# Attention pipeline of a two-layer decoder trunk: weight units parted one per quarter, two query copies for three, the heads' normalisation shared by ScalarE and GpSimd

## The chip, the cores and the metric

The kernel runs on one core of a Trainium2 chip. The metric is the time of one execution on the device, in microseconds (us): the median of the runs. A core has engines that work side by side, each through its own instructions in order, and wait for each other by semaphores: TensorE (PE in the profile, its weight loads PEld), VectorE (DVE), ScalarE (ACT), GpSimd (POOL), and SyncE (SP), which issues the DMAs here. TensorE writes its results to PSUM, from where VectorE and ScalarE fetch them.

## The reference

A trunk of two layers over 256 positions of width 1024, in float32, batch 1. Each layer is half a SwiGLU, a mixer, half a SwiGLU, each between RMS norms. The first layer's mixer is a causal pooling, the second's an attention whose keys and values come from the residual stream after the first layer. What the change touches is this mixer:

```python
def dilated_mixer(h, cos, sin, w_q, k_sh, v_sh, w_o):
    q = (h @ w_q).reshape(B, S, N_ATTN_GROUPS, HEADS_PER_GROUP, HEAD_DIM)   # 3 groups, 8 heads, 64
    q = apply_rope(q, cos, sin)
    for g, (window, dilation) in enumerate(ATTN_GROUPS):
        o, l = dilated_window_attention(q[:, :, g], k_sh[:, :, g], v_sh[:, :, g], window, dilation)
    ...
    wts = jax.nn.softmax(jnp.stack(lses, axis=0), axis=0)
    o = jnp.sum(wts[..., None] * jnp.stack(outs, axis=0).astype(jnp.float32), axis=0)
    return o.reshape(B, S, O_WIDTH) @ w_o
```

Each group has its own mask (which keys a query sees). Weighting the three outputs by the softmax of their log denominators is the same as one softmax over the keys of all three groups together, and the kernel computes that.

## The kernel before, in words

Float32 products are made from two rounded halves: every weight and every activation is split into a high part and a residual, and three matmuls (high by high, high by residual, residual by high) make one product. So every piece of weight that is loaded passes through ScalarE, which casts the high part (L99), and VectorE, which subtracts it to get the residual (L100). `parts(raw, k)` does this for one unit: half of a loaded buffer of two units. A unit of the query weights is 768 columns wide, a unit of all other weights 1024. Loaded buffers (`raw`) come in three, formed units (`hl`) in six, with two more in a pool `xy`.

The attention stage comes after the keys and values are projected. The positions lie in two tiles of 128 rows (`i` = 0, 1), the eight heads in four pairs (`pr` = 0 to 3), and a pair has an even head (`e` = 0) and an odd one (`e` = 1). For each `pr` and `i` there are these steps:

- `q_proj(pr, i, half)`: projects the queries of a pair for all three groups (384 columns) in two halves of two units each; after the second half, `rope` on VectorE (L658 to L662: product, two half products, sum).
- `q_turn(pr, i)`: three transposes on TensorE (`qtp`), copied by ScalarE to the transposed queries `qT` (L772).
- `scores(pr, i)`: the scores of both heads on TensorE (`sc`), on VectorE the mask and the row maximum (L710), on ScalarE the exponential with the row sum `den` (L714; the profile shows the reading of the sum as an instruction of its own, ACTIVATION_READ_ACCUMULATOR).
- `over_sums(pr, i)`: for each head the reciprocal of the sum on VectorE (L720), and the probabilities `p` scaled by it in place on GpSimd (L721).
- `p_turn(pr, i)`: four transposes for each head on TensorE (`ptp`), each head's copied by ScalarE (L737).
- `values(pr, i)`: sixteen matmuls with the values (`ob`), whose result goes to `oT`, high part by ScalarE (L748), residual by VectorE (L749).
- `next_q(pr, k)`, called once in each quarter k of a `pr`: loads the weights of the next pair (the output weights in the last `pr`) and forms their units.

The loop over `pr` mixes the steps of neighbouring pairs, written out by hand. A `pr` issues in this order: `q_proj(pr,0,0)`, `over_sums(pr-1,0)`, `q_turn(pr-1,1)`, `p_turn(pr-2,1)`, `next_q(pr,0)`, `q_proj(pr,0,1)`, `scores(pr-1,1)`, `values(pr-2,1)`, `p_turn(pr-1,0)`, `next_q(pr,1)`, `q_proj(pr,1,0)`, `over_sums(pr-1,1)`, `q_turn(pr,0)`, `values(pr-1,0)`, `next_q(pr,2)`, `q_proj(pr,1,1)`, `scores(pr,0)`, `next_q(pr,3)`. After the loop come the output projection `o_proj` and the last steps of the last pairs. The loop lies in a region (`manual_schedule`) in which TensorE, VectorE and ScalarE issue the region's instructions in the order in which the code emits them; GpSimd and the DMA queue are ordered by the compiler's scheduler, which also decides where instructions from outside the region (the first weight units of the next SwiGLU, for one) fall between them.

Of the kernel before, what the change touches and what calls it, by code (L numbers as in the profile page):

```python
# [19 lines left out]
P = 128  # L20
# [27 lines left out]
def trunk_kernel(ctx: ExitStack, tc: tile.TileContext, x, pos, gains, pscale, ws, wq, invf, amask, pmat, icnt, out):  # L48
    nc = tc.nc
# [36 lines left out]
    def load_raw(pool=rawp, tag="raw", raw=None, at=None):  # L86

        b = block_no[0]
        raw = pool.tile([P, 2, 1024], F32, tag=tag, name=f"{tag}{b}") if raw is None else raw
        for k in range(2) if at is None else (at,):  # L90
            last["dma"] = nc.sync.dma_start(raw[:, k], ws[b, :, k * 1024 : (k + 1) * 1024])
        block_no[0] += at != 0
        return raw

    def parts(raw, k, n=1024, xy=False):

        pool, tag = (xyp, "xy") if xy else (hlp, "hl")
        hl = pool.tile([P, 2, 1024], F32R, tag=tag, name="hl")
        nc.scalar.copy(hl[:, 0, :n], raw[:, k, :n])  # L99
        last["dve"] = nc.vector.tensor_sub(hl[:, 1, :n], raw[:, k, :n], hl[:, 0, :n])  # L100
        return hl[:, 0], hl[:, 1]
# [8 lines left out]
    def load_units(n, xy=False):  # L110

        units = []
        for b in range(n // 2):
            raw = load_raw()
            units += [parts(raw, k, xy=xy and b == 0) for k in range(2)]
        return units
# [1 line left out]
    def load_form():  # L118
        return form(load_raw())

    def load_q_units(pr, b):
        raw = rawp.tile([P, 2, 1024], F32, tag="raw", name=f"rawq{pr}{b}")
        nc.sync.dma_start(raw[:, :, :768], wq[pr * 2 + b])
        return [parts(raw, k, 768, pr % 2 == 0 and b == 0) for k in range(2)]

    def mm(o, l, r, start, stop):
        nc.tensor.matmul(o, l, r, start=start, stop=stop)  # L127
# [357 lines left out]
    with tc.manual_schedule(engines={mybir.EngineType.DVE, mybir.EngineType.Activation}):  # L485
        y = norm(0, gpre, "x")
        raws = [load_raw(at=0)]
# [59 lines left out]
    raw = rawp.tile([P, 2, 1024], F32, tag="raw", name="rawpm")  # L547
# [4 lines left out]
    units = load_units(8, True)  # L552
# [58 lines left out]
    units = load_units(8, True)  # L611
# [41 lines left out]
    def rope(src, i, nh, name):  # L653
        r = sc2.tile([P, nh, 2, 32], F32, tag="w2", name=f"ra_{name}")
        b = sc2.tile([P, nh, 2, 32], F32, tag="w2", name=f"rb_{name}")
        s4 = src.rearrange("p (h two d) -> p h two d", two=2, d=32)
        c4 = ctab[:, i : i + 1].to_broadcast([P, nh, 2, 32])
        nc.vector.tensor_mul(r, s4, c4)  # L658
        for z in range(2):
            sz = stab[:, i, z : z + 1].to_broadcast([P, nh, 32])  # L660
            nc.vector.tensor_mul(b[:, :, z], s4[:, :, 1 - z], sz)
        nc.vector.tensor_add(r, r, b)  # L662
        return r.rearrange("p h two d -> p (h two d)")
# [6 lines left out]
    for g in range(3):  # L670
        units = load_units(4, g % 2 == 0)
        for i in range(2):
            ps = gup.tile([P, 512], F32, tag="gu", name=f"kp{g}{i}")
            proj_mm(ps, hkT, i, units, 512)
            r = rope(ps, i, 8, f"k{g}{i}")
            tp = tpp.tile([P, 4, P], F32, tag="tp", name=f"ktp{g}{i}")
# [3 lines left out]
    for g in range(3):  # L680
        units = load_units(4, g % 2 == 1)
# [5 lines left out]
    qx = [s8p.tile([P, 2, 1024], F32, tag="s8", name=f"qT{k}") for k in range(2)]  # L687
    qx.append(s4p.tile([P, 2, 512], F32, tag="s4", name="qT2"))
    qT = [qx[g // 2][:, g % 2].rearrange("p (r s) -> p r s", r=4) for g in range(3)]
    am = qx[2][:, 0].bitcast(BF16).rearrange("p (i k) -> p i k", i=2)  # L690
    pTt = [t.rearrange("p (c t) -> p c t", c=4) for t in (qx[1][:, 1, 0:512], qx[1][:, 1, 512:1024], qx[2][:, 1])]
    nc.gpsimd.dma_start(am, amask.rearrange("i p k -> p i k"))
# [3 lines left out]
    def scores(pr, i, pool=accp, tag="acc"):  # L696

        q = [t[:, pr] for t in qT]
        t = slice(i * P, (i + 1) * P)
        sc = [pool.tile([P, 512], F32, tag=tag, name=f"sc{i}_{pr}{e}") for e in range(2)]  # L700
        for o, g, keys in ((0, 0, slice(0, S)), (256, 1, t), (384, 2, t)):
            for e in range(2):
                a = slice(e * 64, e * 64 + 64)
                n = keys.stop - keys.start
                mm(sc[e][:, o : o + n], q[g][a, t], kT[g][a, pr, keys], True, True)
        probs[i, pr] = []
        for e in range(2):
            p = sc2.tile([P, 512], F32, tag="w2", name=f"p{i}_{pr}{e}")
            mx = st.tile([P, 1], F32, tag="mx", name=f"mx{i}_{pr}{e}")
            nc.vector.tensor_tensor_reduce(p, sc[e], am[:, i], 1.0, -3.0e38, op0=ALU.add, op1=ALU.max, accum_out=mx)  # L710
            nm = st.tile([P, 1], F32, tag="nm", name=f"nm{i}_{pr}{e}")
            nc.vector.tensor_scalar_mul(nm, mx, -0.125)
            den = st.tile([P, 1], F32, tag="den", name=f"den{i}_{pr}{e}")
            nc.scalar.activation(p, p, AF.Exp, bias=nm, scale=0.125, accum_out=den)  # L714
            probs[i, pr].append((p, den))

    def over_sums(pr, i):
        for e, (p, den) in enumerate(probs[i, pr]):
            rd = st.tile([P, 1], F32, tag="rd", name=f"rd{i}_{pr}{e}")
            nc.vector.reciprocal(rd, den)  # L720
            nc.gpsimd.tensor_scalar_mul(p, p, rd)  # L721
            probs[i, pr][e] = p

    oT = [None, None]
# [3 lines left out]
    def p_turn(pr, i):  # L728

        pT[i, pr] = []  # L730
        for e in range(2):
            tp = tpp.tile([P, 4, P], F32, tag="tp", name=f"ptp{i}_{pr}{e}")
            for c in range(4):
                nc.tensor.transpose(tp[:, c], probs[i, pr][e][:, c * P : (c + 1) * P], ident)
            pT[i, pr].append(pTt[npt[0] % len(pTt)])
            npt[0] += 1
            nc.scalar.copy(pT[i, pr][e], tp)  # L737
# [15 lines left out]
    def o_proj(i, chunks):  # L753
        if chunks[0] == 0:
            acc_f[i] = acc_pair(f"o{i}")
        for k in chunks:
            row_mm(acc_f[i], oT[i][:, 0, k], oT[i][:, 1, k], units[k], k == 0, k == 3)

    def q_proj(pr, i, half, units):
        if half == 0:  # L760
            qp[i] = accp.tile([P, 512], F32, tag="acc", name=f"qp{pr}{i}")
        for q in (2 * half, 2 * half + 1):
            proj_mm(qp[i][:, :384], aT, i, units, 384, only=q)
        if half == 1:
            qr[pr, i] = rope(qp[i][:, :384], i, 6, f"q{pr}{i}")

    def q_turn(pr, i):
        tp = gup.tile([P, 4, P], F32, tag="gu", name=f"qtp{pr}{i}")
        for c in range(3):
            nc.tensor.transpose(tp[:, c], qr[pr, i][:, c * P : (c + 1) * P], ident)  # L770
        for g in range(3):
            nc.scalar.copy(qT[g][:, pr, i * P : (i + 1) * P], tp[:, g])  # L772

    qp, qr = {}, {}
    units = []

    def next_q(pr, k):

        if k % 2 == 0:
            units.extend(load_q_units(pr + 1, k // 2) if pr < 3 else load_units(2))  # L780

    with tc.manual_schedule(engines={mybir.EngineType.PE}):
        with tc.manual_schedule(engines={mybir.EngineType.DVE, mybir.EngineType.Activation}):
            units += load_q_units(0, 0) + load_q_units(0, 1)
            for pr in range(4):
                cur, units = units, []
                q_proj(pr, 0, 0, cur)
                if pr > 0:
                    over_sums(pr - 1, 0)
                    q_turn(pr - 1, 1)  # L790
                if pr > 1:
                    p_turn(pr - 2, 1)
                next_q(pr, 0)
                q_proj(pr, 0, 1, cur)
                if pr > 0:
                    scores(pr - 1, 1)
                if pr > 1:
                    values(pr - 2, 1)
                if pr > 0:
                    p_turn(pr - 1, 0)  # L800
                next_q(pr, 1)
                q_proj(pr, 1, 0, cur)
                if pr > 0:
                    over_sums(pr - 1, 1)
                q_turn(pr, 0)
                if pr > 0:
                    values(pr - 1, 0)
                next_q(pr, 2)
                q_proj(pr, 1, 1, cur)
                scores(pr, 0)  # L810
                next_q(pr, 3)
        o_proj(0, (0,))
        over_sums(3, 0)
        q_turn(3, 1)
        o_proj(0, (1, 2))
        p_turn(3, 0)
        scores(3, 1, gup, "gu")
        values(3, 0)
        p_turn(2, 1)
        o_proj(0, (3,))  # L820
        over_sums(3, 1)
        go.first(0, acc_f[0])
        o_proj(1, (0,))
        values(2, 1)
        o_proj(1, (1,))
        p_turn(3, 1)
        go.second(0)
        o_proj(1, (2,))
        values(3, 1)
        o_proj(1, (3,))  # L830
# [131 lines left out]
```

## Time and profile before

| | us |
|---|---|
| median of 3 runs | 984.12 (982.98 to 987.3) |
| the profiled execution | 985.76 |
| its span, first to last instruction | 984.0 |
| TensorE busy in the span | 950.4 (97%) |
| VectorE busy | 684.1 (70%) |
| ScalarE busy | 542.9 (55%) |
| GpSimd busy | 62.3 (6%) |

The profile is one execution. Busy is the time in which an engine worked on an instruction; matmuls are pipelined, so a busy TensorE is not one at its peak. The attention loop runs from 699 to about 790 us of the span.

### The profile page before, as it was taken

The numbers are of one execution on the slowest core, as the hardware profiler recorded it, in microseconds if no ns is written. First come the engines' busy times: TensorE is split into PE (matmuls) and PEld (weight loads), VectorE is DVE, ScalarE is ACT, GpSimd is POOL, SyncE is SP. The second block draws the span as 40 slices with busy tenths as digits, with TensorE's granted clock in tenths as the row PEclk, the third lists the DMA queues.
The fourth block names the chain that finished last, engine by engine and source line by source line (L and its number), as shares of the span: only waits on it lengthen the run. The fifth ranks groups of instructions, "written<-read, shape, count | busy, mean of one in ns | idle before, by whom it ended". The sixth has DMA issues, their size and how long they took to land.

```text
span 984.0 us, 12092 instructions
## 1 busy us (share of the span) xinstructions
PE 950.4 (97%) x4560; PEld 783.7 (80%) x4560; DVE 684.1 (70%) x771; ACT 542.9 (55%) x693; POOL 62.3 (6%) x66
## 2 busy tenths in 40 slices
PE   7999999999999999999999999999987899999997
PEld 6888788878788878877888888788976778887886
DVE  5979874577788886458887964785465587887642
ACT  6665753455657565347656743644345576665531
POOL 0000000000100000000000000100033310000000
PEclk8999999999999999999999999999999799999999
DMA  7886876475468687546687765564324236967721
GB/s 248 286 266 205 259 260 207 173 227 187 164 211 265 181 280 261 179 139 213 153 317 218 268 243 175 177 217 139 127 95 153 86 107 194 330 163 260 247 90 43
DMA packets 55898, 197.16 MB, mean 200 GB/s; under 512 B 7392, under 2 KB 7392, under 8 KB 53792
## 3 DMA queue, kind: packets, MB, share of 16 engines
q1 hardware_dynamic: 53456, 179.35, 52.2%
q0 software_dynamic: 2384, 17.04, 8.9%
q8 instruction: 36, 0.59, 0.2%
q14 instruction: 22, 0.18, 0.0%
HBM read 178.54 MB, written 1.05 MB: 183 GB/s over the span
## 4 chain that ended last, share of the span: by engine, by line
PE 74%; DVE 11%; ACT 5%; DMA 4%; issue 3%; POOL 2%; SPq 0%; POOLq 0%; DVEq 0%; ACTq 0%
PE acc_d L127 22%; PE g L127 12%; PE st L314 12%; PE u L127 7%; PE acc_b L127 6%; PE vp L127 3%; DVE hl L100 3%; PE kp L127 3%; DMA xy<-raw 2%; DVE hl_lo L107 2%; PE htp L295 2%; ACT hl L99 2%; PE qp L127 1%; DVE h L193 1%; PE acc_w L127 1%
## 5 line engine op out<-in xcount | busy, mean ns | idle before, releaser
L100 DVE TENSOR_TENSOR hl<-raw,hl 128x1024 fp32r<-128x1024 f32 x182 | 221.0, 1222 | 111.6 <-ACT hl L99 110.5
L99 ACT CAST hl<-raw 128x1024 fp32r<-128x1024 f32 x182 | 189.7, 1051 | 138.3 <-PE acc_d L127 103.3
L127 PE MATMUL acc_d<-hl,h 128*128 128x512 f32 x1056 | 243.5, 390 | 0.0
L127 PEld LDWEIGHTS acc_d<-hl,h 128*128 128x128 f32 x1056 | 197.3, 188 | 40.4
L107 DVE TENSOR_TENSOR hl_lo<-xy,hl_hi 128x2048 fp32r<-128x2048 f32 x40 | 91.6, 2291 | 48.6 <-ACT hl_hi L106 48.6
L107 DVE TENSOR_TENSOR hl_lo<-raw,hl_hi 128x2048 fp32r<-128x2048 f32 x48 | 109.4, 2285 | 15.6 <-ACT hl_hi L106 15.5
L106 ACT CAST hl_hi<-xy 128x2048 fp32r<-128x2048 f32 x40 | 76.5, 1913 | 64.0 <-DVE xy L333 29.7
L106 ACT CAST hl_hi<-raw 128x2048 fp32r<-128x2048 f32 x48 | 91.9, 1914 | 20.8 <-PE st L314 10.6
L127 PE MATMUL acc_b<-hl,aT_m 128*128 128x512 f32 x192 | 44.8, 392 | 0.3 <-ACT aT_m L205 0.3
L127 PEld LDWEIGHTS acc_b<-hl,aT_m 128*128 128x128 f32 x192 | 35.7, 188 | 8.3 <-ACT aT_m L205 0.8
L127 PE MATMUL g<-hl_hi,aT_m 128*128 128x512 f32 x128 | 41.9, 393 | 0.0
L127 PE MATMUL u<-hl_hi,aT_m 128*128 128x512 f32 x128 | 41.8, 393 | 0.0
L314 PE MATMUL st<-hl_hi,S_m 128*128 128x512 f32 x128 | 41.8, 393 | 0.0
L127 PE MATMUL qp<-hl,aT_f 128*128 128x384 f32 x192 | 38.9, 354 | 0.0
L297 ACT CAST h<-htp 128x512 fp32r<-128x512 f32 (+1 forms) x48 | 26.2, 548 | 20.0 <-PE htp L295 20.0
L127 PEld LDWEIGHTS qp<-hl,aT_f 128*128 128x128 f32 x192 | 34.8, 198 | 1.3 <-issue 0.8
L127 PE MATMUL kp<-hl,aT_hk 128*128 128x512 f32 x144 | 34.6, 394 | 0.0
L331 POOL DMA_DIRECT2D xy<-raw x16 | 14.1, 878 | 305.2 <-DVE xy L333 82.3
L127 PE MATMUL vp<-hl,aT_hk 128*128 128x512 f32 x144 | 33.1, 390 | 0.0
L314 PE MATMUL st<-hl_hi,aT_m 128*128 128x512 f32 x96 | 31.6, 393 | 1.3 <-ACT hl L99 0.9
L721 POOL TENSOR_SCALAR p<-p,rd 128x512 f32<-128x512 f32 x16 | 24.9, 1566 | 121.9 <-DVE rd L720 100.1
L298 DVE TENSOR_TENSOR h<-htp,h 128x512 fp32r<-128x512 f32 (+1 forms) x48 | 30.6, 640 | 1.1 <-ACT h L297 1.0
(246 smaller groups left out, 1596.4 us busy)
## 6 DMA issues: line engine op xcount, KB each, us to landing
raw<-in_ws SPq DMA_DIRECT2D x278, 512.0 KB, 4.8
xy<-in_ws SPq DMA_DIRECT2D x32, 512.0 KB, 6.8
xy<-raw POOLq DMA_DIRECT2D x16, 1024.0 KB, 8.1
rawq<-in_wq SPq DMA_DIRECT2D x8, 768.0 KB, 4.7
gain_post<-in_gains SPq DMA_DIRECT2D x14, 256.0 KB, 5.0
gain_pre<-in_gains SPq DMA_DIRECT2D x12, 256.0 KB, 6.1
rawpm<-in_pmat SPq DMA_DIRECT2D x2, 512.0 KB, 4.1
out_dram<-h SPq DMA_DIRECT2D x4, 256.0 KB, 2.1
```

Source lines behind the costliest of these rows:

```text
L99: nc.scalar.copy(hl[:, 0, :n], raw[:, k, :n])
L100: last["dve"] = nc.vector.tensor_sub(hl[:, 1, :n], raw[:, k, :n], hl[:, 0, :n])
L106: nc.scalar.copy(hi, raw)
L107: last["dve"] = nc.vector.tensor_sub(lo, raw, hi)
L127: nc.tensor.matmul(o, l, r, start=start, stop=stop)
L193: nc.vector.scalar_tensor_tensor(h[i][:, c], y[:, c], rs, h[i][:, c], op0=ALU.mult, op1=ALU.add)
L295: nc.tensor.transpose(tp[:, k], prod[c, i][:, k * P : (k + 1) * P], ident)
L297: nc.scalar.copy(d[:, 0], tp[:, :nt])
L298: nc.vector.tensor_sub(d[:, 1], tp[:, :nt], d[:, 0])
L314: nc.tensor.matmul(ps, a(z, k), u[v], start=start and k == 0 and n == 0, stop=k == 3 and n == 2, skip_group_check=not start,)
L331: nc.gpsimd.dma_start(dst, src, accum_op=ALU.add)
L721: nc.gpsimd.tensor_scalar_mul(p, p, rd)
```

## The change

`next_q` formed both units of a buffer in the quarters 0 and 2 and nothing in 1 and 3; it now loads the buffer in the quarters 0 and 2 and forms one unit in each quarter. The copies of two of the three query groups, whose targets lie in one tile, become one instruction. The scaling of the odd head's probabilities goes from GpSimd to ScalarE.

```diff
-    def load_q_units(pr, b):
+    def load_q_raw(pr, b):
         raw = rawp.tile([P, 2, 1024], F32, tag="raw", name=f"rawq{pr}{b}")
         nc.sync.dma_start(raw[:, :, :768], wq[pr * 2 + b])
-        return [parts(raw, k, 768, pr % 2 == 0 and b == 0) for k in range(2)]
+        return raw
+
+    def q_parts(raw, pr, k):
+        return parts(raw, k % 2, 768, pr % 2 == 0 and k < 2)
...
+    q01 = qx[0].rearrange("p g (r s) -> p g r s", r=4)
...
             nc.vector.reciprocal(rd, den)
-            nc.gpsimd.tensor_scalar_mul(p, p, rd)
+            if e == 0:
+                nc.gpsimd.tensor_scalar_mul(p, p, rd)
+            else:
+                nc.scalar.mul(p, p, rd)
...
-        for g in range(3):
-            nc.scalar.copy(qT[g][:, pr, i * P : (i + 1) * P], tp[:, g])
+        t = slice(i * P, (i + 1) * P)
+        nc.scalar.copy(q01[:, :, pr, t], tp[:, :2])
+        nc.scalar.copy(qT[2][:, pr, t], tp[:, 2])
...
         if k % 2 == 0:
-            units.extend(load_q_units(pr + 1, k // 2) if pr < 3 else load_units(2))
+            raws[0] = load_q_raw(pr + 1, k // 2) if pr < 3 else load_raw()
+        units.append(q_parts(raws[0], pr + 1, k) if pr < 3 else parts(raws[0], k % 2))
...
-            units += load_q_units(0, 0) + load_q_units(0, 1)
+            for k in range(4):
+                if k % 2 == 0:
+                    raws = [load_q_raw(0, k // 2)]
+                units.append(q_parts(raws[0], 0, k))
```

## Rows read from the trace of the kernel before

**Rows 1.** Windows: length, then for each engine the busy time and the instructions, the granted clock of TensorE (1.00 is full), the DMA share and GB/s.

```profile
699.00:790.00 91.00, 79.98 (x532) 69.61 (x531) 52.56 (x130) 47.85 (x108) 26.14 (x18) 0.91 0.31 107
760.00:764.00 4.00, 3.75 (x20) 3.22 (x21) 0.47 (x5) 2.44 (x8) 3.11 (x2) 0.50 0.37 149
```

**Rows 2.** Waits of TensorE from 695 to 800 us: who waited for whom, us in total, times, the longest.

```profile
PE ob L127 <- ACT qT L737: 6.1, 3, 2.6
PE ptp L734 <- POOL p L721: 2.7, 3, 1.3
```

**Rows 3.** TensorE in order of time: start, length, line, operation, tiles, count; in brackets the idle time before it and what ended it.

```profile
721.43 2.46 PE L127 MATMUL ob<-qT,kv 128*64 128x128 f32 x16 [2.22 <-ACT qT L737]
...
734.32 1.09 PE L127 MATMUL ob<-qT,kv 128*64 128x128 f32 x16
...
760.25 2.46 PE L127 MATMUL ob<-qT,kv 128*64 128x128 f32 x16 [2.65 <-ACT qT L737]
762.64 3.78 PE L127 MATMUL qp<-hl,aT_f 128*128 128x384 f32 x12
...
773.85 0.66 PE L734 MATMUL ptp<-ident,p 128*128 128x128 f32 x4 [1.33 <-POOL p L721]
775.39 0.66 PE L734 MATMUL ptp<-ident,p 128*128 128x128 f32 x4 [0.89 <-POOL p L721]
```

**Rows 4.** ScalarE in order of time, in the third `pr`, columns as in rows 3.

```profile
730.69 0.19 ACT L714 ACTIVATION_READ_ACCUMULATOR p<-p,nm 128x1 f32 x1
730.78 0.58 ACT L772 COPY qT<-qtp 128x128 f32<-128x128 f32 x3
731.24 1.10 ACT L737 COPY qT<-ptp 128x512 f32<-128x512 f32 x2
732.19 1.60 ACT L99 CAST hl<-rawq 128x768 fp32r<-128x768 f32 x2
...
739.25 0.19 ACT L714 ACTIVATION_READ_ACCUMULATOR p<-p,nm 128x1 f32 x1
...
739.49 1.07 ACT L737 COPY qT<-ptp 128x512 f32<-128x512 f32 x2
...
741.90 1.57 ACT L99 CAST hl<-rawq 128x768 fp32r<-128x768 f32 x2
```

**Rows 5.** VectorE in order of time, the same stretch.

```profile
733.10 1.83 DVE L100 TENSOR_TENSOR hl<-rawq,hl 128x768 fp32r<-128x768 f32 x2 [2.04 <-ACT hl L99]
734.85 0.55 DVE L658 TENSOR_TENSOR ra_q<-qp,ctab 128x384 f32<-128x384 f32 x1
...
742.77 1.83 DVE L100 TENSOR_TENSOR hl<-rawq,hl 128x768 fp32r<-128x768 f32 x2 [0.44 <-ACT hl L99]
744.52 0.55 DVE L658 TENSOR_TENSOR ra_q<-qp,ctab 128x384 f32<-128x384 f32 x1
```

**Rows 6.** Groups of instructions by line and form from 660 to 815 us: count, busy us in total, mean ns of one, idle time before them and what ended it.

```profile
L721 POOL TENSOR_SCALAR p<-p,rd 128x512 f32<-128x512 f32 x16 | 24.9, 1566 | 121.9 <-DVE rd L720 100.1 <-ACT qT L737 15.0 <-PE qtp L770 6.9
L100 DVE TENSOR_TENSOR hl<-raw,hl 128x1024 fp32r<-128x1024 f32 x20 | 24.2, 1222 | 9.9 <-ACT hl L99 9.6
L99 ACT CAST hl<-raw 128x1024 fp32r<-128x1024 f32 x20 | 20.7, 1054 | 4.5 <-DVE rb_k L661 2.0 <-PE vp L127 1.4 <-PE qp L127 0.4
...
L100 DVE TENSOR_TENSOR hl<-rawq,hl 128x768 fp32r<-128x768 f32 x16 | 15.3, 983 | 18.4 <-ACT hl L99 18.4
...
L258 ACT ACTIVATE n_m<-n_m,rs_qm 128x512 f32<-128x512 f32 x2 | 1.4, 722 | 2.2 <-POOL rs_qm L178 2.2
```

**Rows 7.** GpSimd in order of time, two pairs of scalings.

```profile
730.44 3.11 POOL L721 TENSOR_SCALAR p<-p,rd 128x512 f32<-128x512 f32 x2 [6.85 <-PE qtp L770]
...
772.23 3.11 POOL L721 TENSOR_SCALAR p<-p,rd 128x512 f32<-128x512 f32 x2 [8.83 <-DVE rd L720]
```

**Rows 8.** ScalarE in order of time: the reading of the second head's sum, with which four other pairs of exponentials end.

```profile
713.18 0.19 ACT L714 ACTIVATION_READ_ACCUMULATOR p<-p,nm 128x1 f32 x1
...
749.42 0.18 ACT L714 ACTIVATION_READ_ACCUMULATOR p<-p,nm 128x1 f32 x1
...
759.38 0.19 ACT L714 ACTIVATION_READ_ACCUMULATOR p<-p,nm 128x1 f32 x1
...
772.42 0.19 ACT L714 ACTIVATION_READ_ACCUMULATOR p<-p,nm 128x1 f32 x1
```

**Rows 9.** VectorE in order of time: residuals and the ropes behind them in the other half-steps, and one reciprocal.

```profile
707.51 1.83 DVE L100 TENSOR_TENSOR hl<-rawq,hl 128x768 fp32r<-128x768 f32 x2 [2.10 <-ACT hl L99]
709.26 0.55 DVE L658 TENSOR_TENSOR ra_q<-qp,ctab 128x384 f32<-128x384 f32 x1
...
714.62 2.26 DVE L100 TENSOR_TENSOR hl<-rawq,hl 128x768 fp32r<-128x768 f32 x2 [1.05 <-ACT hl L99]
716.81 0.55 DVE L658 TENSOR_TENSOR ra_q<-qp,ctab 128x384 f32<-128x384 f32 x1
...
754.32 0.55 DVE L658 TENSOR_TENSOR ra_q<-qp,ctab 128x384 f32<-128x384 f32 x1
...
766.46 0.56 DVE L658 TENSOR_TENSOR ra_q<-qp,ctab 128x384 f32<-128x384 f32 x1
...
771.90 0.17 DVE L720 RECIPROCAL rd<-den 128x1 f32<-128x1 f32 x1
```

**Rows 10.** DMA issues of the page, the query weights: count, KB each, median us from issue to landing.

```profile
rawq<-in_wq SPq DMA_DIRECT2D x8, 768.0 KB, 4.7
```

## The prediction

> **What bounds the kernel now.** I read the page first, then the table of windows, then the waits of TensorE in the attention stage, and then the rows of each engine there in order of time. In the windows the reader is to see that from 699 to 790 us TensorE is busy for 79.98 of 91 us, so 11 us are idle, and that ScalarE and VectorE are each busy for about half of it [rows 1]. Nobody is saturated; work goes round between engines. The waits say how: 6.1 us of the idle time is the value product `ob` waiting for ScalarE's copy of the transposed probabilities, 2.7 us is the transposes of probabilities waiting for GpSimd's scaling [rows 2]. A wait of over 2 us costs twice: the `ob` behind the 2.22 and 2.65 us waits takes 2.46 us, an undisturbed one 1.09 [rows 3], and the stretch from 760 to 764 us has a granted clock of 0.50, the lower of the two levels (1.2 GHz) [rows 1].
>
> ScalarE and VectorE work in the order in which the code issues. The rows show it: the copies of transposed queries (L772) start at 730.78, when the exponentials are through, though their transposes are long done, and the rope at 734.85 starts when the second weight residual (733.10, two of them, 1.83 us) is off VectorE, though its projection was done earlier: the scores issued behind it are already over when `ob` starts at 734.32 [rows 3 to 5]. So the clock of this stage is the chain that runs through both queues from one pair of exponentials to the next rope. I call that stretch a half-step and measure it from the end of the second exponential's accumulator read to the first rope product. Kind A goes from `scores(pr,0)` to the rope of `q_proj(pr+1,0,1)`, kind B from `scores(pr-1,1)` to that of `q_proj(pr,1,1)`.
>
> **The change, part by part.** The total of casts, residuals and scalings stays. What counts is where they stand in the two queues.
>
> *Kind A.* Before, for pr 1 to 2: exponentials through at 730.69 + 0.19 = 730.88; query copies from 730.78, probability copies from 731.24, two casts from 732.19, two residuals from 733.10, rope at 734.85 [rows 4, 5]. That is 3.97 us. After, `next_q(pr,3)` puts a cast and a residual in front of `over_sums(pr,0)`. On VectorE the two reciprocals stand behind that residual, and on ScalarE the new scaling of the odd head waits for its reciprocal, with the query copies, probability copies and the next cast queued behind it. With E for the end of the exponentials: cast at E - 0.10 (as the copy starts now), residual 0.91 later (732.19 to 733.10) at E + 0.81, through at E + 1.77 (0.96 each: 1.83 for two that overlap by 0.1; the 768-wide mean is 983 ns [rows 6]); reciprocals, 0.16 us [rows 9], through by E + 1.95; scaling from E + 2.0. Its price is that of the same form at L258, 722 ns [rows 6], of which about 0.62 delays the next ScalarE instruction, since neighbours overlap by some 0.1: E + 2.62. Two query copies for three: 0.46 us now (730.78 to 731.24); a copy of twice 128 columns lies between a third of 0.58 and half of 1.10 (0.19 to 0.55 [rows 4]), I take 0.38, near the shorter, and 0.43 for both: E + 3.05. Probability copies 0.95 (731.24 to 732.19): E + 4.0. Cast, then residual 0.91 later: E + 4.9; only one residual now stands before the rope, 0.88: E + 5.78. The half-step grows by **1.8 us**: 2.7 us added in front, 0.9 saved behind.
>
> TensorE needs the unit that is late by E + 1.77 in the second half of `q_proj`; it will wait there for a microsecond or so, but that lies beside the longer chain and costs nothing more.
>
> *Kind B*, pr = 2. Before: E = 739.25 + 0.19 = 739.44, probability copies from 739.49, `ob`, casts from 741.90, residuals from 742.77, rope at 744.52: 5.08 us. The `ob` round trip leaves ScalarE a hole. After: copies through at E + 1.0, cast, residual at E + 1.87, through at E + 2.83; reciprocals E + 3.0; scaling E + 3.05 to 3.67; query copies E + 4.10; `oT` copy E + 4.26; cast; residual E + 5.13; rope E + 6.01. **Plus 0.9 us**: the hole hides the rest. `ob` itself, through at about E + 2.3, is no longer last.
>
> *All half-steps.* Before the first, the rope of `q_proj(0,1,1)` stood behind two residuals (707.51, 1.83 us; rope 709.26); behind one it starts at 708.39: **-0.87**. A for pr 0 to 1 has no probability copies: before 713.18 + 0.19 to 716.81, 3.44; after 5.78 - 0.95 = 4.83: **+1.4** [rows 8, 9]. B for pr 1: the `ob` of 721.43 took 2.46 instead of 1.09, and this 1.37 covers the 0.9: **0**, or +0.9 if its clock holds [rows 3]. A 1 to 2 **+1.8**, B for pr 2 **+0.9**, A 2 to 3 (749.42 + 0.18 to 754.32, with units of the next layer's weights in both) **+1.8**. B for pr 3, 759.38 + 0.19 to 766.46, 6.89: with 1024 wide units (1054 and 1222 ns) the same sum gives E + 6.9, and TensorE's slow projection (762.64, 3.78 us) ends there as well: **0** [rows 3, 6, 8, 9].
>
> *Tail.* E = 772.61. Now the odd head's transposes start at 775.39 and end at 776.05, E + 3.44, after two GpSimd scalings of 1.56 in a row [rows 3, 7, 8]. After: the last output unit is cast at E - 0.1, its residual runs from E + 1.0 to 2.2, the reciprocal follows, GpSimd starts 0.33 behind that (771.90 to 772.23) at E + 2.45 and ends at E + 4.0; ScalarE has done the odd head long before; eight transposes to E + 5.25: **+1.8**. One GpSimd turn (1.56) is saved here, but the unit in front takes 2.3 us, and the even head's reciprocal no longer runs beside the second exponential.
>
> Sum: -0.87 + 1.4 + 0 + 1.8 + 0.9 + 1.8 + 0 + 1.8 = +6.8 us. TensorE's waits grow by as much, and one more stretch at the lower clock is likely; 1.37 us each, at least half of it hidden beside the chain, so +0.7 (between 0 and two whole ones, +2.7). In all **+7.5 us**. Against the profiled execution, 985.76 us, that is 993.3; that execution was 1.6 above the median, and I forecast on the median: 984.1 + 7.5 = **991.6 us**.
>
> *Costed at nothing.* GpSimd's own time: it is busy for 26.14 of 91 us [rows 1]. The input buffers: each of three is held a quarter longer, but the load that waits for one is due a whole `pr` later, some 17 us, and lands in 4.7 [rows 10]. If that cover failed, each late load would cost the missing part of 4.7 us.
>
> One residual pair ran 2.26 us instead of 1.83 while GpSimd scaled (714.62), the pair of 733.10 did not although GpSimd was at work as well until 733.55 [rows 5, 7, 9]. The Trainium skill (GPSIMD Engine Reference, Key points) says that GpSimd shares its SBUF interfaces with VectorE and that instructions with two SBUF inputs contend. By the rule, half of GpSimd's time gone would give back something at every residual; by the rows it is 0.43 us at one place, inside the first A, and the sum would be +7.1 by it.
>
> **Rivals.** *The shorter pieces win (faster).* Each rope stands behind one residual instead of two, 0.88 us earlier in every half-step, and the odd head is off GpSimd. If the reciprocals were not held by the residual in front (the order on VectorE being other than the code's), A would change by +0.62 for the scaling and -1.6 for the cast and residual moved behind, about -1.0; over the six half-steps after the first rope and with 0.87 there -6.9, less what TensorE then bounds (11 us idle, [rows 1]): about 979 us. For it: the waits of [rows 2] would all shrink. Against it: the strict order that [rows 4, 5] show. The Trainium skill says as much as this rival (Perfetto Trace Analysis, Optimizing Scalar/DVE Operations): where these engines are not saturated but cause bubbles, breaking up instructions may let work finish sooner. Here the pieces are not only smaller, half of them move to the front of a chain. Chance 0.06.
>
> *The chain is covered.* The next layer's units (cast 1.05, residual 1.22) that now run between the exponentials and ropes fall into ScalarE's new waits for the reciprocal, over 1 us in each half-step: two such units hidden give back about 4.5, and 988 us, inside 0.5%. For it: the order of these is not the code's. Against: VectorE has no such hole. Chance 0.16.
>
> *The clock falls at every new wait.* TensorE waits in the middle of `q_proj` and again before `ob`; with each of the three `pr` at the lower clock, 3 x 1.37 to 3 x 2.5 more: 996 to 999 us. For it: waits of 2.22 and 2.65 did so [rows 3]. Against: a chain of the other engines hides a slow TensorE. Chance 0.15. The forecast keeps 0.63.
>
> **The numbers.** About 0.5% (5 us) is what a measurement of this kernel can tell from no change. Faster has its rival, 0.06; same is the covered chain, 0.16, less a little of it that ends above 989, plus the low end of the forecast: 0.15; slower 0.79. The range goes from 985.5 (three units hidden) to 998.5 (the clock falling at nearly each wait).
>
> **What would show it.** Right: VectorE's L720 starts behind an L100 in each half-step, ScalarE sits idle for about a microsecond before each new scaling, ended by L720; kind A near 5.8 and B near 6.0 us; `qp` appears among TensorE's waits, on L100; the first transposes of the last `pr` wait on GpSimd for over 3 us; the stage from 699 ends about 7 us later, and nothing before it moves. Wrong: L720 ahead of the residual, half-steps shorter than 4 and 5 us, or TensorE's waits below 11 us in this stage.

## The result, and the profile after

The changed kernel takes 987.29 us (median of 20 executions) beside 984.33 for the kernel before in the same runs: a ratio of 1.0026 (95% interval 1.0017 to 1.0036), slower by 2.6 us by that ratio. Taken again it was 986.59, ratio 1.0018 (1.0005 to 1.0031). The direction was forecast, the size was not: 7.5 us had been worked out. By the prediction's own measure of 5 us this counts as no change, to which it gave 0.15. Three of the first 20 executions (1351 to 5390 us), the profiled one among them, were disturbed, so the profile below is that of the second measurement (execution 986.59 us, span 984.8). Line numbers stand a few higher than before: L724 is the reciprocal, L726 the scaling on GpSimd, L728 the one on ScalarE, L661 the rope's first product, L718 the exponential, L779 and L780 the copies of the transposed queries, L741 the transposes of the probabilities, L744 the copy of the transposed probabilities.

TensorE's waits in the attention stage of the changed kernel, from 695 to 800 us (compare [rows 2]): us in total, times, the longest.

```profile
PE ob L130 <- ACT qT L744: 7.3, 3, 3.6
PE ob L130 <- DVE mx L714: 2.1, 1, 2.1
PE qp L130 <- DVE hl L100: 1.1, 2, 0.6
PE tp_m L206 <- DVE n_m L259: 0.9, 1, 0.9
PE qp L130 <- ACT hl L99: 0.9, 2, 0.6
```

And ScalarE's, from 705 to 775 us:

```profile
ACT p L718 <- DVE nm L716: 22.7, 7, 3.7
ACT p L728 <- DVE rd L724: 7.6, 6, 1.5
```

The new wait is there, six times, 1.2 to 1.5 us each, and the projection waits for its late units (1.1 and 0.9). The wait of `ptp` for GpSimd, 2.7 us in [rows 2], is gone.

Now the same half-steps as in [rows 4, 5], kind A of the third `pr`. ScalarE in order of time:

```profile
730.52 0.18 ACT L718 ACTIVATION_READ_ACCUMULATOR p<-p,nm 128x1 f32 x1
730.61 0.82 ACT L99 CAST hl<-rawq 128x768 fp32r<-128x768 f32 x1
732.65 0.72 ACT L728 ACTIVATE p<-p,rd 128x512 f32<-128x512 f32 x1 [1.22 <-DVE rd L724]
733.28 0.35 ACT L779 COPY qT<-qtp 128x256 f32<-128x256 f32 x1
733.53 0.27 ACT L780 COPY qT<-qtp 128x128 f32<-128x128 f32 x1
733.69 1.08 ACT L744 COPY qT<-ptp 128x512 f32<-128x512 f32 x2
734.65 0.86 ACT L99 CAST hl<-rawq 128x768 fp32r<-128x768 f32 x1
```

VectorE beside it:

```profile
731.46 0.96 DVE L100 TENSOR_TENSOR hl<-rawq,hl 128x768 fp32r<-128x768 f32 x1 [1.61 <-ACT hl L99]
732.34 0.22 DVE L724 RECIPROCAL rd<-den 128x1 f32<-128x1 f32 x2
735.54 0.96 DVE L100 TENSOR_TENSOR hl<-rawq,hl 128x768 fp32r<-128x768 f32 x1 [2.98 <-ACT hl L99]
736.42 0.55 DVE L661 TENSOR_TENSOR ra_q<-qp,ctab 128x384 f32<-128x384 f32 x1
```

From 730.70 (730.52 + 0.18) to 736.42 are 5.72 us; 5.78 were worked out. The scaling costs 0.72, the copy of two query groups 0.35 for the 0.38 taken. All half-steps, from the two traces (end of the second exponential's accumulator read to the first rope product, in us):

| | before | after | grew | forecast |
|---|---|---|---|---|
| A, 0 to 1 | 3.44 | 4.73 | 1.3 | 1.4 |
| B, pr 1 | 5.78 | 5.86 | 0.1 | 0 |
| A, 1 to 2 | 3.97 | 5.72 | 1.7 | 1.8 |
| B, pr 2 | 5.08 | 6.16 | 1.1 | 0.9 |
| A, 2 to 3 | 4.72 | 6.19 | 1.5 | 1.8 |
| B, pr 3 | 6.89 | 6.99 | 0.1 | 0 |

So the loop does what was forecast: the last rope starts 4.4 us later, counted from the first query projection, where 5.0 were worked out. What gave time back lies behind it. From that rope to the end of the pair of exponentials: 6.15 us before, 4.30 after (-1.85), since the two residuals of the next SwiGLU's weights that ran there (the second between the row maximum and its scaling by -0.125) have moved. VectorE before:

```profile
767.46 1.22 DVE L100 TENSOR_TENSOR hl<-raw,hl 128x1024 fp32r<-128x1024 f32 x1
769.67 1.22 DVE L100 TENSOR_TENSOR hl<-raw,hl 128x1024 fp32r<-128x1024 f32 x1
```

In every kernel below in which the units are parted, this stretch takes 4.1 to 4.4 us; in every one in which they are not, 6.1 to 6.2. From these exponentials to the end of the output projection: 22.3 before, 20.1 after (-2.2); forecast +1.8. Behind that +1.0, and -0.6 ahead of the loop. The sum, 4.4 - 1.85 - 2.2 + 1.0 - 0.6, is the 0.8 us between the spans of the two profiled executions; the medians of the runs differ by more (1.3 and 3.0).

The tail in the changed kernel. VectorE:

```profile
773.66 0.16 DVE L724 RECIPROCAL rd<-den 128x1 f32<-128x1 f32 x1
774.63 0.17 DVE L724 RECIPROCAL rd<-den 128x1 f32<-128x1 f32 x1 [0.81 <-ACT p L718]
775.58 1.23 DVE L100 TENSOR_TENSOR hl<-raw,hl 128x1024 fp32r<-128x1024 f32 x1 [0.78 <-ACT hl L99]
```

TensorE:

```profile
773.02 3.00 PE L130 MATMUL acc_o<-hl,oT 128*128 128x512 f32 x12
775.87 1.03 PE L741 MATMUL ptp<-ident,p 128*128 128x128 f32 x8
776.83 1.15 PE L130 MATMUL sc<-kv,qT 64*128 64x256 f32 x12
780.04 1.09 PE L130 MATMUL ob<-qT,kv 128*64 128x128 f32 x16 [2.07 <-DVE mx L714]
781.07 1.09 PE L741 MATMUL ptp<-ident,p 128*128 128x128 f32 x8
```

The reader sees both reciprocals ahead of the residual, the first even before the second exponential is through. GpSimd's one scaling lies beside the output projection, and the eight transposes follow without a wait, where those of 773.85 and 775.39 waited 1.33 and 0.89 us [rows 3]. They end 2.3 us after the exponentials (774.60), where before it was 3.44: -1.1. Where +1.8 was forecast, the turn of GpSimd that is saved shows nearly whole, since no residual stands in front of the reciprocals, as none did before.

The rest of the -2.2 is something else. TensorE never falls to the lower clock here: from 770 to 795 us the granted clock is 1.00, and `ob` and the transposes behind it take 1.09 us each. Before, from 776 to 783 us, it was 0.51:

```profile
775.98 2.08 PE L127 MATMUL sc<-kv,qT 64*128 64x256 f32 x12
778.93 1.97 PE L127 MATMUL ob<-qT,kv 128*64 128x128 f32 x16 [0.88 <-DVE mx L710]
780.84 1.97 PE L734 MATMUL ptp<-ident,p 128*128 128x128 f32 x8
```

These three took 2.7 us more than in the changed kernel. Against that, `ob` now waits 2.07 us for the row maximum instead of 0.88, behind a residual of a moved unit (VectorE, 778.06 to 779.28), and some 0.4 more is lost behind it. But the change is not shown to be what kept the clock up. The kernel before with nothing but the query copies changed (e10 below) waits for GpSimd as the kernel before does, and keeps a granted clock of 1.00 from 774 to 781 us:

```profile
772.40 0.66 PE L735 MATMUL ptp<-ident,p 128*128 128x128 f32 x4 [1.36 <-POOL p L722]
773.94 0.66 PE L735 MATMUL ptp<-ident,p 128*128 128x128 f32 x4 [0.89 <-POOL p L722]
774.52 1.15 PE L127 MATMUL sc<-kv,qT 64*128 64x256 f32 x12
776.55 1.09 PE L127 MATMUL ob<-qT,kv 128*64 128x128 f32 x16 [0.88 <-DVE mx L711]
```

Its tail takes 20.0 us, like the changed kernel's. The clock differs between executions of one kernel as well: over 56 executions of the kernel before, beside the experiments, the mean granted clock goes from 0.985 (times from 985.8 to 987.9 us) to 0.994 (981.7 us). The profiled one had 0.986. So 0.8 us between two single profiles understates the change; the medians count.

The microsecond behind is most likely the next stage's start; no experiment isolates it. In the changed kernel the norm of the first tile waits longer: two residuals of weights (789.08, 2.35 us) now stand on VectorE ahead of the small sum from which the row's scale comes (before at 789.10, ahead of them):

```profile
789.08 2.35 DVE L100 TENSOR_TENSOR hl<-raw,hl 128x1024 fp32r<-128x1024 f32 x2
791.35 0.15 DVE L179 SCALAR_TENSOR_TENSOR ms_qm<-ss_qm 128x1 f32<-128x1 f32 x1
```

### The profile page after: what moved, and what is told of

Read it like the earlier page. It is cut to its first block, busy times and chain, and to the rows that moved or that the text cites. A ratio compares the mean times of both kernels' runs of the same rounds, so it can differ in the third digit from the quotient of the medians.

```text
span 3073.0 us, 12063 instructions
## 1 busy us (share of the span) xinstructions
PE 3064.6 (100%) x4560; PEld 1696.6 (55%) x4560; DVE 701.0 (23%) x771; ACT 554.9 (18%) x693; POOL 48.3 (2%) x58
## 4 chain that ended last, share of the span: by engine, by line
PE 100%; DVE 0%; ACT 0%; DVEq 0%; POOLq 0%; issue 0%; ACTq 0%
PE acc_d L130 26%; PE st L317 17%; PE g L130 14%; PE acc_b L130 10%; PE u L130 10%; PE kp L130 4%; PE vp L130 3%; PE qp L130 3%; PE acc_u L130 3%; PE acc_w L130 3%; PE htp L298 2%; PE acc_o L130 1%; PE sc L130 1%; PE yp L130 1%; PE tp_f L206 1%; PE ob L130 1%
## 5 line engine op out<-in xcount | busy, mean ns | idle before, releaser
L130 PE MATMUL acc_d<-hl,h 128*128 128x512 f32 x1056 | 815.7, 1035 | 0.0
L130 PEld LDWEIGHTS acc_d<-hl,h 128*128 128x128 f32 x1056 | 432.0, 410 | 367.5 <-issue 364.7
L130 PE MATMUL acc_b<-hl,aT_m 128*128 128x512 f32 x192 | 137.8, 968 | 0.0
L130 PE MATMUL kp<-hl,aT_hk 128*128 128x512 f32 x144 | 121.9, 1117 | 0.0
L317 PE MATMUL st<-hl_hi,S_m 128*128 128x512 f32 x128 | 111.7, 974 | 0.0
L130 PE MATMUL u<-hl_hi,aT_m 128*128 128x512 f32 x128 | 111.2, 971 | 0.0
L130 PE MATMUL g<-hl_hi,aT_m 128*128 128x512 f32 x128 | 111.0, 972 | 0.0
L130 PE MATMUL acc_w<-hl,yT 128*128 128x512 f32 x96 | 81.1, 1098 | 0.0
L130 PE MATMUL acc_u<-hl,aT_f 128*128 128x512 f32 x96 | 80.4, 1105 | 0.0
L130 PE MATMUL acc_b<-hl,aT_x 128*128 128x512 f32 x96 | 79.9, 1102 | 0.0
```

The costliest lines, as they stand in the source:

```text
L317: nc.tensor.matmul(ps, a(z, k), u[v], start=start and k == 0 and n == 0, stop=k == 3 and n == 2, skip_group_check=not start,)
```

## The experiments

Each is timed beside the kernel before on the same chip; ratios are to that. The edits are to the changed kernel where nothing else is said.

**The changed kernel again.**

> The changed kernel itself, for a profile of an execution that nothing disturbed. Theory Q (the queues as predicted, and units given back): kind A half-steps of 5.8 us and kind B of 6.0 for the third pr, ScalarE idle for about 1 us before each new scaling, qp waiting on L100; the missing 4 us or so come back in the last pr, where units of the next SwiGLU no longer stand between the exponentials and the ropes. Theory S (short): the half-steps grew by less than half of what was worked out (A below 4.9, B below 5.5), and the last pr is no better than before. Time 987 in both.

Measured: the table above. Theory Q holds for the half-steps and the new wait. That the last `pr` gives back is right in the sum and only half right in the cause: 1.85 us by the units and 2.2 by the tail, most of which is the clock of one profiled execution.

**The parts alone**, each put into the kernel before. First the scaling:

```diff
-            nc.gpsimd.tensor_scalar_mul(p, p, rd)
+            if e == 0:
+                nc.gpsimd.tensor_scalar_mul(p, p, rd)
+            else:
+                nc.scalar.mul(p, p, rd)
```

> Before, with only the odd head's scaling on ScalarE. Theory Q: the reciprocal stands right behind its exponential, so the scaling adds some 0.8 us to each kind A half-step, nothing to kind B (the hole of ob takes it), and saves 1.1 us in the tail: about +1.5 us over before, 985.8. Theory S or any theory in which the parts add up: whatever is missing to the changed kernel when the split alone is taken off, so mul and split together +3.

985.03 us, ratio 0.9997 (0.9984 to 1.0011): no change. A for pr 1 to 2 is 4.92 for 3.97, as expected; B for pr 2 is 6.14 for 5.08, which was not. There the granted clock is 0.50 from 743 to 746 us, and the projection behind `ob` takes 3.91 us instead of 2.38. Why it fell is not shown: e10 below has the same B at 6.15 and a low clock there, with an A no longer than before (3.90). The tail gives it back, at 19.3 us for 22.3.

Then the units parted one per quarter, GpSimd scaling both heads and three query copies:

> Before, with only the units parted one per quarter (GpSimd scales both heads, three query copies). Theory Q: without the scaling on ScalarE nothing there waits for the residual in front, half-steps A 3.8 and B 4.2 us (0.1 and 0.9 shorter than before), the tail 2.8 us longer; in all 984 to 985, no change. With e2 that leaves 5 us of the predicted 6.8 to the two parts together. Theory S: the parts add, e2 and e3 give +3 between them.

982.15 us, ratio 0.9961 (0.9947 to 0.9975): faster, where no change was expected. A was right (3.82), B for pr 2 is 4.59 where 4.2 was expected. The tail was the same error as in the prediction: 0.7 us longer than before where 2.8 was expected, with both reciprocals ahead of the residual again. The stretch ahead of it gives back 1.9 us by the moved units.

The copies:

```diff
-        for g in range(3):
-            nc.scalar.copy(qT[g][:, pr, i * P : (i + 1) * P], tp[:, g])
+        t = slice(i * P, (i + 1) * P)
+        nc.scalar.copy(q01[:, :, pr, t], tp[:, :2])
+        nc.scalar.copy(qT[2][:, pr, t], tp[:, 2])
```

> Before, with only the two query copies for three. Theory Q: 0.1 us less on ScalarE before each rope, where kind A is bound by it, and nothing in kind B: 0.3 us in all, no change that can be measured (984 to 986 beside the same runs of before).

982.71 us, ratio 0.9987 (0.9972 to 1.0002), no change that can be told, as expected.

So the three parts alone are at 0.9997, 0.9961 and 0.9987, and together at 1.0018 to 1.0026. They don't add: some 7 us arise only when the scaling stands on ScalarE and a residual stands ahead of its reciprocal.

**The order of two small instructions.** VectorE's residual of the odd quarters' units is issued behind the reciprocals of `over_sums`, in six places of the loop (a seventh, in the tail, had that order already); nothing else is moved:

```diff
             probs[i, pr][e] = p
+        while late:
+            late.pop()()
...
-        last["dve"] = nc.vector.tensor_sub(hl[:, 1, :n], raw[:, k, :n], hl[:, 0, :n])
+        def residual():
+            last["dve"] = nc.vector.tensor_sub(hl[:, 1, :n], raw[:, k, :n], hl[:, 0, :n])
+
+        if wait:
+            late.append(residual)
+        else:
+            residual()
```

> The changed kernel with one thing exchanged in the order of VectorE: the two reciprocals of over_sums now stand in front of the residual of the unit in the odd quarter, not behind it (six places; everything else on every engine keeps its order). Theory Q: ScalarE no longer waits for the residual, half-steps A of 4.4 (now 5.7) and B of 4.7 us (now 6.2), together 5 to 7 us: 980 to 982, below the kernel before. Theory W (it is the work that moved to ScalarE, cast and scaling, that makes the half-steps long, not the wait): A stays above 5.2, time within 2 us of the changed kernel.

979.94 us, ratio 0.9950 (0.9935 to 0.9965): 5 us under the kernel before, about 7 under the changed one. Theory W falls: A is 4.38 and B 4.72. The tail takes the same 20.1 us as in the changed kernel; the loop, from the first query projection to the last rope, takes 64.5 us for 71.5. The same half-step as above, ScalarE and then VectorE of this kernel (L733 is the reciprocal, L104 the residual, L737 the scaling):

```profile
728.04 0.82 ACT L101 CAST hl<-rawq 128x768 fp32r<-128x768 f32 x1
728.77 0.72 ACT L737 ACTIVATE p<-p,rd 128x512 f32<-128x512 f32 x1
```

```profile
728.17 0.16 DVE L733 RECIPROCAL rd<-den 128x1 f32<-128x1 f32 x1 [0.63 <-ACT p L727]
728.89 0.96 DVE L104 TENSOR_TENSOR hl<-rawq,hl 128x768 fp32r<-128x768 f32 x1 [0.56 <-ACT hl L101]
```

The scaling follows the cast at once, and ScalarE's wait of 7.6 us is gone from its table. The work is the same; only the wait was dear. A new wait shows in the same table, 2.9 us for loads of weights (0.4 in the changed kernel).

**The tail in the code's order.** The prediction had the residual ahead of the reciprocals in the tail too. This edit, which moves the three calls into the region, puts them so:

```diff
-        o_proj(0, (0,))
-        over_sums(3, 0)
-        q_turn(3, 1)
+            o_proj(0, (0,))
+            over_sums(3, 0)
+            q_turn(3, 1)
```

> The changed kernel with the tail's first steps (output projection of one chunk, over_sums of the last pair, its query copies) moved into the region in which VectorE and ScalarE keep the code's order. That is the order which the prediction assumed there. Theory Q with this correction: the last output unit's residual comes before the reciprocals again, so from the end of the last-but-one exponentials to the first transposed probability it takes 4.1 us, where the changed kernel takes 1.3; at most a low clock behind it: 3 to 5 us over the changed kernel, 990 to 991, which is the prediction's number. Theory U (it was the units of the next SwiGLU that gave the time back, not the order of the tail): within 1 us of the changed kernel.

991.94 us, ratio 1.0072 (1.0052 to 1.0093), 5 us over the changed kernel. Theory U falls as the whole account: the moved units stay moved here, and the time is gone. TensorE, VectorE and GpSimd in that tail:

```profile
778.73 1.30 PE L741 MATMUL ptp<-ident,p 128*128 128x128 f32 x8 [4.41 <-POOL p L726]
779.97 2.08 PE L130 MATMUL sc<-kv,qT 64*128 64x256 f32 x12
```

```profile
773.71 1.23 DVE L100 TENSOR_TENSOR hl<-raw,hl 128x1024 fp32r<-128x1024 f32 x1 [1.82 <-ACT hl L99]
774.85 0.22 DVE L724 RECIPROCAL rd<-den 128x1 f32<-128x1 f32 x2
774.99 2.34 DVE L100 TENSOR_TENSOR hl<-raw,hl 128x1024 fp32r<-128x1024 f32 x2
```

```profile
775.20 3.47 POOL L726 TENSOR_SCALAR p<-p,rd 128x512 f32<-128x512 f32 x1 [8.41 <-DVE rd L724]
```

The transposes start 6.0 us behind the exponentials (772.74), not 4.1, and 1.3 in the changed kernel: the residual, reciprocal and scaling start where they were put (GpSimd at E + 2.46, worked out 2.45), but the scaling takes 3.47 us instead of 1.57. The granted clock from 779 to 787 us is 0.57, so a part of the 5 us is the clock. The time is the prediction's number partly by luck: 1.9 us too long here and 1.85 us given back by the moved units, which this kernel keeps, cancel.

**The odd head on VectorE**, first in the kernel before (for GpSimd), then in the changed one, whose edit this is:

```diff
-                nc.scalar.mul(p, p, rd)
+                nc.vector.tensor_scalar_mul(p, p, rd)
```

> Before, with only the odd head's scaling on VectorE: the units stay in pairs, three query copies. Theory Q: VectorE has a hole behind the reciprocals in kind A and B, so the half-steps stay 4.0 and 5.1, and the tail saves the second GpSimd turn, 1.1 us: 982 to 984. If parting the units is what makes e4 fast, this must stay 5 us or more above e4 (977.9); a rival, that VectorE in place of GpSimd alone does it, expects 979 or less.

981.08 us, ratio 0.9958 (0.9943 to 0.9973). Half-steps 3.96 and 5.07, as expected. The tail takes 18.9 us: 3.5 less than in the kernel before, but 1.1 less than in e10, whose clock stayed high there too. That 1.1 is the GpSimd turn that was worked out.

> The changed kernel with the odd head's scaling on VectorE in place of ScalarE: same work, same place in the code, but ScalarE no longer waits for the reciprocal. Theory Q: half-steps as in the split alone (A 3.8, B 4.2), the tail 1.8 longer than before: 983 to 984, some 3 to 4 us under the changed kernel. Theory S: the wait was no matter, so within 1 us of the changed kernel.

977.94 us, ratio 0.9919 (0.9902 to 0.9935), 9 us under the changed kernel where 3 to 4 were expected: A 3.77 and B 4.78 as worked out within 0.6. The miss is the tail, 18.4 us at the full clock, where 1.8 more than the 22.3 of before had been expected.

> e4 (odd head scaled on VectorE) with the reciprocals in front of the residual as in e6. Theory Q: nothing on ScalarE waits for the reciprocals here, the exchange only brings the probabilities earlier, for which nobody waits but the transposes behind GpSimd, and sets the residual 0.5 us later: within 1 us of e4, 977 to 979. Theory W: no difference either, but then e6 doesn't gain.

976.46 us, ratio 0.9917 (0.9900 to 0.9934): no difference from e4, as expected. Nobody on ScalarE waits for a reciprocal here.

> The changed kernel with both heads scaled on VectorE, GpSimd with nothing. Theory Q: 0.5 us more on VectorE in each half-step, where it has a hole in kind A (it waits for a cast), and 1 us less in the tail, where the transposes wait for GpSimd: within 1.5 us of e4.

977.95 us, ratio 0.9937 (0.9917 to 0.9957), 1.8 us above e4 by the ratios where 1.5 was expected, with intervals that overlap. These three beat both kernels, and parting the units is a gain in them: 0.9919 with it (e4), 0.9958 without (e9). That is less than the 5 us that e9 had asked of parting the units, and more than its rival, by which VectorE alone does it, allows; both have a share.

## Why the prediction was wrong in size

*Right:* the waits that bound the stage, the strict order of both queues within the loop, and the growth of each half-step to 0.3 us. A unit's cast and residual moved ahead of `over_sums`, the reciprocal stood behind the residual and ScalarE behind the reciprocal; e6 shows that this alone is worth 7 us. The rival in which the shorter pieces win was right about its condition, the reciprocals ahead: e6 is faster. Its 979 us beside the measured 979.9 is luck, though. It had every half-step shorter by about 1.0 us; in e6, A is 4.38, longer than the 3.97 of before, and the six half-steps together are 1.8 us shorter, not 6. The rest comes from the first rope, the moved units and the tail.

*The step that failed* is the tail: "the last output unit is cast at E - 0.1, its residual runs from E + 1.0 to 2.2, the reciprocal follows", +1.8 us. The region with the code's order ends with the loop; `over_sums(3,0)` stands behind it, and there the scheduler put the reciprocals first. The transposes are through at E + 2.3, not E + 5.25: -1.1 us in place of +1.8. (The whole tail measured -2.2, with the clock in it.) I had the order from rows of the loop and used it past the loop's end. e5, which makes the assumed order true, is slower by 5 us.

*The clock term* (+0.7) did not come. Low clocks in the loop did not become more (two stretches in either kernel), and the one in the tail, which cost 2.7 us in the profiled execution of the kernel before, is absent; e10 shows that it can be absent with the old waits too. Nor does every wait of over 2 us cost twice, as the prediction had from two rows: in e9 an `ob` behind a wait of 2.36 us takes 1.57 us, at a granted clock of 1.00 (720 to 725 us).

*Cover that was there:* the rival of the covered chain, 988 us at 0.16, is where the time landed, and half of its reason holds, for 1.85 us: units of the next SwiGLU, which the code does not order, moved out of the chain. They did not fall into ScalarE's new waits, as the rival had it, but into the tail, where one of them makes `ob` wait 1.2 us longer for the row maximum. Against the gain also stands the 1.0 us at the next stage's start, which no case had.

*Costed at nothing, rightly:* the buffers held a quarter longer (ScalarE's waits for a load are 0.4 us in the changed kernel), and the parts' bare work. In the faster kernels with parted units that cover is thinner: ScalarE waits 2.9 to 4.3 us for loads in e3, e4, e6, e7 and e8.

## What to carry to other kernels

When a large instruction is cut and a piece moved forward, look at what small instruction falls behind it in the same queue, and which engine waits for that one: here 0.16 us reciprocals behind a 0.96 us residual cost ScalarE 1.2 us six times. Moving an instruction to an engine whose queue is strictly ordered makes all that engine's later work wait for its input. An order read from rows holds only as far as the code fixes it; past that edge, let the prediction carry both orders. And before a stretch's gain is put down to a change, compare its granted clock in both profiles, and in a third kernel that leaves the stretch alone.

## What the runs showed of the hardware

GpSimd's scaling of 128x512 takes 1.57 us in most rows, but 3.47 in the row of e5 above, beside two residuals of VectorE that ran one behind the other. In the kernel with the units parted alone a pair of scalings takes up to 4.13 us instead of 3.11, and the two residuals beside it 2.85 instead of 2.34:

```profile
768.10 4.13 POOL L724 TENSOR_SCALAR p<-p,rd 128x512 f32<-128x512 f32 x2 [3.09 <-DVE rd L723]
```

```profile
769.57 2.85 DVE L100 TENSOR_TENSOR hl<-raw,hl 128x1024 fp32r<-128x1024 f32 x2 [0.77 <-ACT hl L99]
```

The Trainium skill (GPSIMD Engine Reference, Key points) has it that GpSimd shares its SBUF interfaces with VectorE and that instructions with two SBUF inputs, as the residual is, contend. These rows agree, and put 1.9 us on it in e5, where two residuals ran one behind the other; the prediction had 0.43 us, from one pair of residuals that took longer while GpSimd scaled.
